# Zero fills on other engines, packed phase powers and a later state-space scan in a hybrid decoder block

## The chip, the cores and the metric

The kernel runs on one core of a Trainium2 chip. The metric is the device time of one execution in microseconds (us); the shown value is the median of three runs. The engines are called by the names of the profile: PE is TensorE, DVE is VectorE, ACT is ScalarE, POOL is GpSimd, SP is the engine that issues the weight loads.

## What is computed

One decoder layer on 512 tokens of width 1024, in float32. Only the parts that the change touches are shown.

```python
def hybrid_mixer(h, w_in, ...):
    proj = h @ w_in
    qa, ka, va, qd, kd, vd, u, g = jnp.split(proj, cuts, axis=-1)
    ya, _ = banded_attention(qa, ka, va, ...)      # branch A: window 128, 8 heads
    yb = dilated_attention(qd, kd, vd)             # branch B: three windows
    yc = s5_mixer(u, lam_re, lam_im, log_dt, ...)  # branch C: state space
    gates = jax.nn.sigmoid(g)
    merged = gates_0 * (ya @ w_branch_a) + gates_1 * (yb @ w_branch_b) + gates_2 * (yc @ w_branch_c)
    return merged @ w_out

def s5_mixer(u, ...):        # 32 groups of 16 channels, 64 complex states each
    ab_re, ab_im = mag * cos(li * dt), mag * sin(li * dt)
    # x_t = Abar x_{t-1} + Bbar u_t ;  y = Re(C x) + D u ;  then GELU and a gated unit
```

After the mixer come a residual, a norm, a gated convolution FFN of width 2816 and a final norm.

## The kernel before, in words

Every float32 weight is split into a high and a low part (`whi` by a copy on ACT, L66; `wlo` by a subtraction on DVE, L92), and each product of the layer is three matmuls (L171 to L173). Weights come in chunks of 256 columns; a chunk serves two **units** of work. A unit is 24 matmuls of 512 columns into one PSUM bank of the tag `mm` (there are two), and an evacuation of that bank on ACT: `pj` (a projection) for units 1 to 6 and 15 to 24, `th` (a gate, L983) for units 7 to 14.

The order of all work is written by hand. Each engine executes its instructions in the order in which the program emits them. `run` goes through the units; before unit u it emits one split of a coming chunk (`whi` on ACT, then `wlo` on DVE) and then the closures that `before(u, ...)` has put there. So a closure that waits on DVE holds up the split of the next unit, and the matmuls behind it.

The state-space branch runs as such closures, for four groups j of channels:

- `ssm_scalars` computes sine and cosine of the phase in tiny DVE instructions, mixed with the evacuations of the first norm (`hTl`, L345).
- `ssm_phase` squares the phase eight times on POOL (tiles `t`) and builds two tables from it (`eb`, `ea`, with the scratch `esc`). `ssm_e(j)` multiplies them to `E` on POOL.
- `ssm_cpow` multiplies the output weights by four powers on POOL (`vt`, `Vw`): three powers at its first step, the fourth at its second.
- `ssm_inj(j)`, `ssm_bd(j)` and `ssm_ob(j)` prepare the matrices. `ob` and `tz` are block-diagonal and must be zero outside the blocks.
- `ssm_m1(j)`: 16 matmuls into both PSUM banks of the tag `sc` (L677); four products `z` on DVE, which free those banks; two sums `z` on POOL; two scans on DVE (L687, L688); four more products on DVE, and `X` on POOL.
- `ssm_m2(j)`: matmuls with `tz`, `ob` and `X` (L711, L713) and the output `yS`.

Branch A (`attn_a`, four blocks of queries) uses the same two `sc` banks for its scores (L757). DVE adds the mask and takes the maximum (L764), ACT takes the exponentials (`smA`, L773), DVE divides. A step is one `st_(A[i])`.

All scratch tiles of 2 KB share one pool of 46 buffers (`slot`). A new tile takes over the buffer of an older one, and its first writer then waits for the last reader of that one.

Of the kernel before, what the change touches and what calls it, by code (L numbers as in the profile page):

```python
# [31 lines left out]
def hybrid_block(  # L32
# [36 lines left out]

# [1 line left out]
    class Chunk:  # L71
        """One raw load of up to [128, 2048] and its pieces of up to [128, 1024]."""

# [27 lines left out]
    def cols(w, c0, nl=1):  # L101
        """256 columns of a [1024, n] weight: eight k tiles in two pieces; get(k, c)."""

        def v(r):
            return r[:, :].rearrange("p (k n) -> p k n", n=256)

        wv = w.rearrange("(k p) n -> p k n", p=128)
        n = KD // nl
        c = Chunk([(lambda r, i=i: v(r)[:, i * n:i * n + n, :], wv[:, i * n:i * n + n, c0:c0 + 256])
                   for i in range(nl)],  # L110
                  [([128, 4, 256], [(lambda t: t[:, :, :], lambda r, i=i: v(r)[:, 4 * i:4 * i + 4, :])], None)
                   for i in range(2)])
        c.get = lambda k, a: tuple(t[:, k % 4, a * 128:a * 128 + 128] for t in c.p[k // 4])
        return c

    def qcols(w, cc):
        """Query columns of branch A, head pairs (j, j + 4) side by side, j = 2cc and 2cc + 1."""

# [17 lines left out]
    def rows(nk, n, loads):  # L136
        """n columns of a weight of nk k tiles, in pieces of 1024 / nk columns; get(k, c)."""
        pc = 1024 // nk

        def v(r):  # L140
            return r[:, :].rearrange("p (k n) -> p k n", n=n)

        c = Chunk([(lambda r, d=d: d(v(r)), s) for d, s in loads],
                  [([128, nk, pc], [(lambda t: t[:, :, :], lambda r, i=i: v(r)[:, :, i * pc:(i + 1) * pc])], None)
                   for i in range(n // pc)])

        def get(k, a):
            o = a * 128 % pc
            return tuple(t[:, k, o:o + 128] for t in c.p[a * 128 // pc])

        c.get = get
        return c

    def krows(w, k0, nk, c0, mk=None):
        """nk k tiles by 512 columns, as the moving operand; get(k)."""

# [24 lines left out]
    def tile_mm(ps, w, c, nk, act, o=slice(0, T)):  # L181
        """One [128, 512] output tile (or the tokens o of it), channels on partitions."""
        for k in range(nk):
            xh, xl = act(k)
            mm3(ps[:, o], w.get(k, c), xh[:, o], xl[:, o], k == 0, k == nk - 1)

# [1 line left out]
    units = []  # (chunk, closure emitting matmuls and evacuation)  # L188
    early = {}  # unit -> (chunk, pieces) to split before it, beyond the next chunk
    later = []  # closures to emit before the next unit  # L190
    plan = {}   # unit -> closures to emit before it

# [60 lines left out]

    queue = []       # small operations that fill the gaps of VectorE
    deferring = [False]
# [25 lines left out]

# [1 line left out]
    mhalf, epsv = cst([128, 1], "mhalf"), cst([128, 1], "epsv")  # L283
# [49 lines left out]
    def to_hT(pair, xs, gcol, dst, tags, hook=lambda: None):  # L333
        """Transposes two scaled token tiles (k -> view) into dst, times the norm's weight."""
        for kk in range(KD // 2):
# [38 lines left out]

# [1 line left out]
    P0_, P1_ = slice(0, 256), slice(256, 512)  # L376
# [20 lines left out]

# [1 line left out]
    maskA = cst([128, 256], "maskA")  # L399
# [23 lines left out]

# [1 line left out]
    cnt = [0]  # L425
# [11 lines left out]
    def exact_exp(o, i):  # L437
        """exp by reduction to |r| <= ln2 / 2 and its series, in float32."""
        c, k, r, p = ex
# [46 lines left out]
    def cmul(o, a, b, t, eng=None):  # L486
        """o = a * b for complex pairs; t: four scratch views."""
        tt(t[0], a[0], b[0], MUL, eng)
        tt(t[1], a[1], b[1], MUL, eng)
        tt(t[2], a[0], b[1], MUL, eng)  # L490
        tt(t[3], a[1], b[0], MUL, eng)
        tt(o[0], t[0], t[1], SUB, eng)
        tt(o[1], t[2], t[3], ADD, eng)

    pcol = cst([128, 48], "pcol")
    lr, li, ld, dcol = pcol[:, 0:16], pcol[:, 16:32], pcol[:, 32:48], vcol2[:, 32:48]
    dt_, mag, sn, cs, ar, ai, fr, fi, mag4 = (tiny() for _ in range(9))
    W, Vw, V0, V0b, DI, eb, ea = [], [], [], [], [], [], []
# [39 lines left out]
    def ssm_phase():  # L538
        ct = [tiny() for _ in range(4)]

        def csq(a):
            o = (tiny(), tiny())
            cmul(o, a, a, ct, G)
            return o

        pw = [csq(csq((cs, sn)))]
        for _ in range(6):
            pw.append(csq(pw[-1]))
        # phases of the chunks: 16 small steps times 8 large ones
        te, ta = slot([128, 2, 16, 16], name="eb"), slot([128, 2, 16, 8], name="ea")  # L550
# [55 lines left out]
    def expand(dst, src, j, scale=None):  # L606
        """Block diagonal over the two groups of each pair."""
        for g in range(2):
# [37 lines left out]

# [1 line left out]
    yS = []  # L648
# [72 lines left out]

# [1 line left out]
    def to_nat(src, name, strided=False):  # L723
        """[128 ch, 512] -> [128 keys, block, 128 ch]; strided: block r has the keys r, r + 4, ..."""
        pb = bank("pt")
# [74 lines left out]

# [1 line left out]
    zh, zl, yc = {}, {}, []  # L802
# [28 lines left out]

# [1 line left out]
    yb = {}  # L833
# [5 lines left out]
    def attn_b(hp):  # L839
        # statistics: [group, block, head of the pair]  # L840
        mx, nm, l = (cst([128, 3, 4, 2], f"{n}{hp}") for n in ("mxB", "nmB", "lB"))
# [24 lines left out]
        for i in range(4):  # L866
            for e in range(2):
                v = P0[i, e]
                S.activation(v, v, AF.Exp, bias=nm[:, 0, i, e:e + 1], scale=SCALE, accum_out=l[:, 0, i, e:e + 1])
        # group 0's statistics in the order of the other groups: (t mod 4, t div 4)  # L870
        nl = cst([128, 4, 2, 2], f"nlB{hp}")
# [102 lines left out]

# [1 line left out]
    m, th = {}, {}  # L976
# [48 lines left out]

# [1 line left out]
    x1 = []  # L1027
# [52 lines left out]

# [1 line left out]
    cpar = cst([128, 4, NF * 2], "cpar")  # L1082
# [62 lines left out]
    def down_unit(chunk, half, k0, n):  # L1145
        def fn():
# [11 lines left out]
            if final:  # L1158
                # the last token's part of this chunk goes to two banks of its own, 256 columns each
                order += [(NT - 1, k, c) for c in (slice(0, 256), slice(256, 512)) for k in range(n)]  # L1160
# [60 lines left out]

# [1 line left out]
    wup = bank("o", name="wup")  # L1223
# [33 lines left out]
    trans1(1, lambda: pump(2))  # L1257
    for j in range(4):
        OB[j] = [slot([128, 4, 4, 2, 16], name="ob") for _ in range(2)]
        TZ[j] = slot([128, 4, 4, 32], name="tz")  # L1260
        for t in (*OB[j], TZ[j]):
            G.memset(t, 0.0)
    masks_dve()
# [81 lines left out]
    before(5, lambda: ssm_inj(1), lambda: ssm_bd(2))  # L1345
    before(6, lambda: ssm_inj(2), lambda: ssm_bd(3), lambda: ssm_m1(0), st_(CP), lambda: ssm_e(1))
    before(7, lambda: ssm_inj(3), st_(A[0]))
    before(8, lambda: VA.append(to_nat(proj["vA"], "VA")), lambda: ssm_ob(0), st_(A[0]))
    before(9, lambda: ssm_m2(0), lambda: ssm_ob(1), lambda: ssm_m1(1), lambda: ssm_e(2))
    before(10, lambda: ssm_ob(2), st_(A[0]), st_(A[1]))  # L1350
    before(11, lambda: ssm_ob(3), st_(A[0]), st_(A[1]))
    before(12, lambda: ssm_m2(1), lambda: ssm_m1(2), lambda: ssm_e(3))
    before(13, st_(A[1]), st_(A[2]))
    before(14, st_(A[1]), st_(A[2]))
    before(15, st_(A[1]), lambda: ssm_m2(2), lambda: ssm_m1(3))
    before(16, st_(A[2]), st_(A[3]))
    before(17, st_(A[2]), st_(A[3]))
    before(18, st_(A[2]), lambda: ssm_m2(3))
    before(19, st_(A[3]))
    before(20, st_(A[3]), lambda: VB.setdefault(0, [to_nat(proj["vB", 0], "VB0")]))  # L1360
    before(21, st_(A[3]), lambda: VB[0].append(to_nat(proj["vB", 0], "VB1", True)))
    before(22, lambda: VB.setdefault(1, [to_nat(proj["vB", 1], "VB0")]))
# [44 lines left out]
```

## Time and profile before

| | before |
|---|---|
| median of three runs | 854.11 us (853.79 to 855.87) |
| profiled execution, first to last instruction (span) | 852.8 us |
| PE busy | 819.5 us, 96% of the span |
| DVE, ACT, POOL busy | 480.1, 352.1, 176.1 us |
| mean granted TensorE clock | 0.983 |

The profiled execution is timed by its span alone; the median of the runs lies 1.3 us above it. PE is busy nearly throughout, so the time can fall where PE stands still or runs at the lower clock.

### The profile page before, as it was taken

The page shows a single profiled execution, that of the slowest core. Times are in us where ns is not written, and L with a number is a line of the kernel's source. Part 1 is how long each engine was busy: PE and PEld are TensorE (multiplying, and loading weights), DVE is VectorE, ACT ScalarE, POOL GpSimd, SP SyncE. Part 2 cuts the span into 40 slices and gives each one's busy share as a digit, 9 for nine tenths or more (in the row PEclk, how much of TensorE's full clock was granted, in tenths as well). Part 3 has the DMA queues.
Part 4 walks back from the last instruction along what each step waited for, and adds up shares of the span by engine and source line. Part 5 has one row for each costly group of instructions (what it writes and reads, how often), then busy time and mean ns, then how long its engine had stood idle before and what let it go on. Part 6 is the DMA issues. An engine that isn't in the chain of part 4 may idle for free.

```text
span 852.8 us, 10536 instructions
## 1 busy us (share of the span) xinstructions
PE 819.5 (96%) x4085; PEld 678.7 (80%) x4085; DVE 480.1 (56%) x913; ACT 352.1 (41%) x661; POOL 176.1 (21%) x245
## 2 busy tenths in 40 slices
PE   8799669999999999999999999999999999999996
PEld 7788556877787788888887898888888888888885
DVE  5996579777224655645474456555566665422313
ACT  6347145445434554442344244444444444312212
POOL 6379876243000000005250000000000000002002
PEclk9899969999999999999999999999999999999999
DMA  8332011111233131332335124222222223323402
GB/s 237 99 99 84 16 50 51 50 49 50 72 77 105 51 99 50 100 99 74 125 100 196 50 64 135 97 91 90 92 91 92 93 98 123 125 72 99 148 0 99
DMA packets 68278, 76.60 MB, mean 90 GB/s; under 512 B 8161, under 2 KB 55557, under 8 KB 68229
## 3 DMA queue, kind: packets, MB, share of 16 engines
q1 hardware_dynamic: 67972, 75.89, 28.3%
q8 instruction: 32, 0.52, 0.3%
q0 software_dynamic: 256, 0.05, 0.1%
q14 instruction: 18, 0.14, 0.1%
HBM read 73.81 MB, written 2.12 MB: 89 GB/s over the span
## 4 chain that ended last, share of the span: by engine, by line
PE 72%; DVE 13%; POOL 8%; issue 3%; ACT 2%; DMA 1%; SPq 0%; POOLq 0%; DVEq 0%; ACTq 0%
PE up L172 9%; PE up L171 9%; PE up L173 9%; PE mm L171 7%; PE mm L172 7%; PE mm L173 7%; PE acc L178 6%; PE acc L179 6%; PE acc L177 6%; POOL t L279 2%; DVE z L279 2%; DVE wlo L92 2%; DVE t L271 1%; POOL esc L279 1%; DVE z L687 1%
## 5 line engine op out<-in xcount | busy, mean ns | idle before, releaser
L92 DVE TENSOR_TENSOR wlo<-raw,whi 128x1024 fp32r<-128x1024 f32 (+1 forms) x126 | 153.1, 1223 | 152.1 <-ACT whi L66 152.0
L66 ACT ACTIVATE whi<-raw 128x1024 fp32r<-128x1024 f32 (+1 forms) x126 | 127.4, 1023 | 58.4 <-PE acc L179 56.2
L171 PE MATMUL up<-hTh,whi 128*128 128x512 f32 (+1 forms) x384 | 142.7, 372 | 0.0
L172 PE MATMUL up<-hTl,whi 128*128 128x512 f32 (+1 forms) x384 | 142.6, 371 | 0.0
L173 PE MATMUL up<-hTh,wlo 128*128 128x512 f32 (+1 forms) x384 | 142.6, 371 | 0.0
L171 PE MATMUL mm<-hTh,whi 128*128 128x512 f32 (+1 forms) x336 | 134.5, 400 | 0.0
L172 PE MATMUL mm<-hTl,whi 128*128 128x512 f32 (+1 forms) x336 | 131.2, 390 | 0.0
L173 PE MATMUL mm<-hTh,wlo 128*128 128x512 f32 (+1 forms) x336 | 130.9, 390 | 0.0
L275 DVE SCALAR_TENSOR_TENSOR cc<-up,cpar,cc 128x511 f32<-128x511 f32 x88 | 65.9, 749 | 97.3 <-ACT cc L1101 95.8
L171 PEld LDWEIGHTS up<-hTh,whi 128*128 128x128 f32 x384 | 72.3, 188 | 12.6
L173 PEld LDWEIGHTS up<-hTh,wlo 128*128 128x128 f32 x384 | 72.3, 188 | 12.6
L172 PEld LDWEIGHTS up<-hTl,whi 128*128 128x128 f32 x384 | 72.3, 188 | 12.3
L171 PEld LDWEIGHTS mm<-hTh,whi 128*128 128x128 f32 x336 | 64.7, 193 | 15.5 <-issue 2.3
L173 PEld LDWEIGHTS mm<-hTh,wlo 128*128 128x128 f32 x336 | 64.4, 192 | 13.2
L172 PEld LDWEIGHTS mm<-hTl,whi 128*128 128x128 f32 x336 | 64.7, 193 | 11.9
L177 PE MATMUL acc<-whi,gh 128*128 128x512 f32 x172 | 66.9, 389 | 0.0
L178 PE MATMUL acc<-wlo,gh 128*128 128x512 f32 x172 | 66.9, 389 | 0.0
L179 PE MATMUL acc<-whi,gl 128*128 128x512 f32 x172 | 66.9, 389 | 0.0
L279 POOL TENSOR_TENSOR x<-x,gfin 128x512 f32<-128x512 f32 x4 | 5.2, 1289 | 296.8 <-ACT acc L1040 296.8
L1101 ACT ACTIVATE cc<-up,cpar 128x512 f32<-128x512 f32 x44 | 34.3, 779 | 61.2 <-PE up L173 60.4
L983 ACT ACTIVATE th<-mm 128x512 f32<-128x512 f32 x24 | 14.2, 594 | 76.2 <-PE mm L173 58.5
L66 ACT ACTIVATE gh<-cc 128x512 fp32r<-128x512 f32 x22 | 13.9, 632 | 59.4 <-DVE cc L279 59.4
(299 smaller groups left out, 1291.2 us busy)
## 6 DMA issues: line engine op xcount, KB each, us to landing
raw<-in_w_up_dram SPq DMA_DIRECT2D x22, 1024.0 KB, 5.1
raw<-in_w_in_dram SPq DMA_DIRECT2D x18, 1024.0 KB, 5.1
raw<-in_w_down_dram SPq DMA_DIRECT2D x10, 1024.0 KB, 5.0
x<-in_x_dram SPq DMA_DIRECT2D x8, 512.0 KB, 6.2
raw<-in_w_in_dram SPq DMA_DIRECT2D x8, 512.0 KB, 5.2
raw<-in_w_out_dram SPq DMA_DIRECT2D x4, 1024.0 KB, 5.1
raw<-in_w_branch_a_dram SPq DMA_DIRECT2D x4, 512.0 KB, 6.7
raw<-in_w_branch_c_dram SPq DMA_DIRECT2D x2, 1024.0 KB, 5.0
```

The costliest lines, as they stand in the source:

```text
L66: S.activation(o, i, AF.Copy)
L92: (lo_eng or V).tensor_tensor(view(lo), r, view(hi).bitcast(F32), op=ALU.subtract)
L171: PE.matmul(ps, wh, xh, start=first, stop=False)
L172: PE.matmul(ps, wh, xl, start=False, stop=False)
L173: PE.matmul(ps, wl, xh, start=False, stop=last)
L177: PE.matmul(ps, xh, wh, start=first, stop=False)
L178: PE.matmul(ps, xh, wl, start=False, stop=False)
L179: PE.matmul(ps, xl, wh, start=False, stop=last)
L275: emit(lambda: V.scalar_tensor_tensor(o, a, s, b, op0=op0, op1=op1))
L279: emit(lambda: (eng or V).tensor_tensor(o, a, b, op=op))
L983: S.activation(t, ps, AF.Tanh, scale=0.5)
L1101: S.activation(dst, ps, AF.Identity, bias=cpar[:, 3, f:f + 1], scale=cpar[:, 2, f:f + 1])
```

## The change

Three edits. The eight `ob` and four `tz` tiles are zeroed at the very start, on DVE (`memset`) and ACT (a copy with scale 0), and no more on POOL after the first norm. The squaring of the phase works on cosine and sine packed side by side: four POOL instructions for a squaring where there were six. And the scans are emitted later: `ssm_m1(0)` moves from unit 6 to unit 9, and each later `ssm_m1`, `ssm_m2` and `ssm_e` three units further on, so that `ssm_m2(3)` stands at unit 21. Comments are taken out as well.

```diff
-    dt_, mag, sn, cs, ar, ai, fr, fi, mag4 = (tiny() for _ in range(9))
+    dt_, mag, ar, ai, fr, fi, mag4 = (tiny() for _ in range(7))
+    cssn = tiny(32)
+    cs, sn = cssn[:, 0:16], cssn[:, 16:32]
...
     def ssm_phase():
-        ct = [tiny() for _ in range(4)]
+        ct, sq = tiny(), tiny(32)
 
         def csq(a):
-            o = (tiny(), tiny())
-            cmul(o, a, a, ct, G)
+
+            o = tiny(32)
+            tt(sq, a, a, MUL, G)
+            tt(ct, a[:, 0:16], a[:, 16:32], MUL, G)
+            tt(o[:, 0:16], sq[:, 0:16], sq[:, 16:32], SUB, G)
+            tt(o[:, 16:32], ct, ct, ADD, G)
             return o
 
-        pw = [csq(csq((cs, sn)))]
+        pk = [csq(csq(cssn))]
         for _ in range(6):
-            pw.append(csq(pw[-1]))
+            pk.append(csq(pk[-1]))
+        pw = [(v[:, 0:16], v[:, 16:32]) for v in pk]
...
+    for j in range(4):
+        OB[j] = [slot([128, 4, 4, 2, 16], name="ob") for _ in range(2)]
+        TZ[j] = slot([128, 4, 4, 32], name="tz")
+        for t in OB[j]:
+            V.memset(t, 0.0)
+        S.activation(TZ[j][:, :, :, :].rearrange("p a b c -> p (a b c)"), epsv.to_broadcast([128, 512]), AF.Copy,
+                     scale=0.0)
     wup = bank("o", name="wup")
...
     trans1(1, lambda: pump(2))
-    for j in range(4):
-        OB[j] = [slot([128, 4, 4, 2, 16], name="ob") for _ in range(2)]
-        TZ[j] = slot([128, 4, 4, 32], name="tz")
-        for t in (*OB[j], TZ[j]):
-            G.memset(t, 0.0)
     masks_dve()
...
-    before(6, lambda: ssm_inj(2), lambda: ssm_bd(3), lambda: ssm_m1(0), st_(CP), lambda: ssm_e(1))
+    before(6, lambda: ssm_inj(2), lambda: ssm_bd(3), st_(CP))
...
-    before(9, lambda: ssm_m2(0), lambda: ssm_ob(1), lambda: ssm_m1(1), lambda: ssm_e(2))
+    before(9, lambda: ssm_m1(0), lambda: ssm_ob(1), lambda: ssm_e(1))
...
-    before(12, lambda: ssm_m2(1), lambda: ssm_m1(2), lambda: ssm_e(3))
+    before(12, lambda: ssm_m2(0), lambda: ssm_m1(1), lambda: ssm_e(2))
...
-    before(15, st_(A[1]), lambda: ssm_m2(2), lambda: ssm_m1(3))
+    before(15, st_(A[1]), lambda: ssm_m2(1), lambda: ssm_m1(2), lambda: ssm_e(3))
...
-    before(18, st_(A[2]), lambda: ssm_m2(3))
+    before(18, st_(A[2]), lambda: ssm_m2(2), lambda: ssm_m1(3))
...
-    before(21, st_(A[3]), lambda: VB[0].append(to_nat(proj["vB", 0], "VB1", True)))
+    before(21, st_(A[3]), lambda: VB[0].append(to_nat(proj["vB", 0], "VB1", True)), lambda: ssm_m2(3))
```

On POOL, between the last weight split of the first norm (`wlo`) and the first squaring, before; the fills in front of these rows repeat the pair `ob`, `tz` four times in all:

```order
L1262 MEMSET ob 128x512 x2
L1262 MEMSET tz 128x512
L279 TENSOR_TENSOR t_669<-t_146 128x16
L279 TENSOR_TENSOR t_670<-t_145 128x16
L279 TENSOR_TENSOR t_671<-t_146,t_145 128x16
L279 TENSOR_TENSOR t_672<-t_145,t_146 128x16
L279 TENSOR_TENSOR t_673<-t_669,t_670 128x16
L279 TENSOR_TENSOR t_674<-t_671,t_672 128x16
```

The same place on POOL with the change:

```order
L92 TENSOR_TENSOR wlo<-raw,whi 128x1024 x2
L279 TENSOR_TENSOR t_669<-t_150 128x32
L279 TENSOR_TENSOR t_668<-t_150 128x16
L279 TENSOR_TENSOR t_670<-t_669 128x16
L279 TENSOR_TENSOR t_670<-t_668 128x16
```

The fills are gone from there, and a squaring is four rows where it was six; eight squarings make 32 instructions where they made 48.

On POOL at the end of the third power of `ssm_cpow`, before (`z` and `X` belong to `ssm_m1(0)`, the last `vt` and `Vw` are the fourth power):

```order
L279 TENSOR_TENSOR Vw<-vt 128x256 x2
L279 TENSOR_TENSOR z<-z 128x512 x2
L696 MEMSET X 128x4 x2
L279 TENSOR_TENSOR X<-z,xt 128x4x127
L279 TENSOR_TENSOR X<-z 128x4x127
L279 TENSOR_TENSOR vt<-Vw,t_147 128x256
L279 TENSOR_TENSOR vt<-Vw,t_148 128x256 x2
L279 TENSOR_TENSOR vt<-Vw,t_147 128x256
L279 TENSOR_TENSOR Vw<-vt 128x256 x2
```

The same place with the change:

```order
L279 TENSOR_TENSOR vt<-Vw,t_145 128x256
L279 TENSOR_TENSOR vt<-Vw,t_146 128x256 x2
L279 TENSOR_TENSOR vt<-Vw,t_145 128x256
L279 TENSOR_TENSOR Vw<-vt 128x256 x2
L279 TENSOR_TENSOR z<-z 128x512 x2
L703 MEMSET X 128x4 x2
```

The fourth power now stands in front of the first scan's sums `z`.

On ACT at units 7 and 8, with the semaphores that each instruction waits for, before (`th` is the evacuation of unit 7, `whi` the next split, `VA` and `ob` belong to unit 8):

```order
L983 ACTIVATE th<-mm 128x512 [waits DVE_49,PE_49]
L66 ACTIVATE whi<-raw 128x1024
L66 ACTIVATE VA<-pt 128x512 [waits PE_49,Pool_49]
L66 ACTIVATE ob<-Vw 64x16x16 [waits Pool_49]
L66 ACTIVATE ob<-Vw 64x16x16
L68 ACTIVATE ob<-Vw 64x16x16 [waits Pool_49]
```

The same place with the change:

```order
L990 ACTIVATE th<-mm 128x512 [waits PE_49,Pool_49]
L66 ACTIVATE whi<-raw 128x1024 [waits DVE_49]
L66 ACTIVATE VA<-pt 128x512 [waits PE_49,Pool_49]
L66 ACTIVATE ob<-Vw 64x16x16 x2
```

The buffers of the pool have moved on: `th` of unit 7 waited for a DVE instruction of the first scan, and now waits for POOL. The count that it waits for is that of the first of the two `Vw` of the fourth power.

## Rows read from the trace of the kernel before

**Rows 1.** Busy time of each engine by stretch, granted clock, DMA

```profile
core 0: us, PE busy (x) PEld busy (x) DVE busy (x) ACT busy (x) POOL busy (x), PEclk, DMA share, GB/s
100.00:110.00 10.00, 1.56 (x9) 1.07 (x8) 7.17 (x7) 1.90 (x3) 5.98 (x9) 0.84 0.00 0
110.00:120.00 10.00, 5.98 (x18) 4.81 (x19) 7.62 (x26) 3.91 (x17) 9.92 (x10) 0.50 0.33 105
600.00:700.00 100.00, 100.00 (x443) 82.81 (x442) 58.08 (x73) 44.18 (x57) 0.00 (x0) 1.00 0.30 95
```

**Rows 2.** Waits of PE up to 240 us: total us, times, longest

```profile
PE sc L757 <- DVE mxA L764: 14.9, 3, 12.5
```

**Rows 3.** DVE in order of time: start, us, instruction, idle before

```profile
0.89 0.17 DVE L312 MEMSET vrow<- 48x128 f32 x1
5.66 0.15 DVE L330 TENSOR_SCALAR stat<-stat 128x1 f32<-128x1 f32 x1 [4.61 <-ACT junk L355]
...
21.86 7.91 DVE L271 TENSOR_SCALAR t<-t 128x16 f32<-128x16 f32 x1
24.10 5.68 DVE L345 SCALAR_TENSOR_TENSOR hTl<-nt,vcol,hTh 128x256 fp32r<-128x256 f32 x1
```

**Rows 4.** POOL in order of time, fills and first squarings

```profile
19.01 5.13 POOL L92 TENSOR_TENSOR wlo<-raw,whi 128x1024 fp32r<-128x1024 f32 x2 [1.57 <-DVE whi L91]
...
29.23 0.51 POOL L1262 MEMSET tz<- 128x512 f32 x1
47.58 0.41 POOL L279 TENSOR_TENSOR t<-t 128x16 f32<-128x16 f32 x2 [17.84 <-DVE t L279]
...
66.11 0.12 POOL L555 MEMSET eb<- 128x16 f32 x1
```

**Rows 5.** POOL in order of time, powers, first scan and a later scan

```profile
97.84 2.36 POOL L279 TENSOR_TENSOR vt<-Vw,t 128x256 f32<-128x256 f32 x4
...
101.54 2.47 POOL L279 TENSOR_TENSOR z<-z 128x512 f32<-128x512 f32 x2
...
111.08 3.34 POOL L279 TENSOR_TENSOR vt<-Vw,t 128x256 f32<-128x256 f32 x4
...
167.73 1.66 POOL L279 TENSOR_TENSOR X<-z,xt 128x508 f32<-128x508 f32 x1 [3.39 <-DVE xt L279]
```

**Rows 6.** DVE in order of time, first two scans and branch A

```profile
102.83 2.27 DVE L687 TENSOR_TENSOR_SCAN z<-a,z 128x512 f32<-128x512 f32 x1 [9.73 <-POOL z L279]
...
115.44 0.28 DVE L764 CUSTOM_DVE_ANT_0 smA<-sc,maskA 128x128 f32<-128x128 f32 x1
...
122.51 2.52 DVE L269 TENSOR_SCALAR smA<-smA,lA 128x128 f32<-128x128 f32 x8
125.24 1.23 DVE L92 TENSOR_TENSOR wlo<-raw,whi 128x1024 fp32r<-128x1024 f32 x1 [0.21 <-ACT whi L66]
...
130.75 2.48 DVE L279 TENSOR_TENSOR z<-sc,E 128x512 f32<-128x512 f32 x4
...
160.37 2.48 DVE L279 TENSOR_TENSOR z<-sc,E 128x512 f32<-128x512 f32 x4
```

**Rows 7.** PE in order of time, units 8 and 9

```profile
114.02 1.64 PE L757 MATMUL sc<-pj 64*128 64x128 f32 x8 [12.46 <-DVE mxA L764]
...
123.47 0.38 PE L711 MATMUL o<-us,tz 128*128 128x128 f32 x2
...
126.14 1.95 PE L677 MATMUL sc<-us,inj 128*128 128x128 f32 x16
```

**Rows 8.** ACT in order of time, first microseconds and evacuations

```profile
4.48 1.06 ACT L355 ACTIVATE junk<-x 128x1024 f32<-128x1024 f32 x1 [2.24 <-DMA x<-in_x_dram]
...
108.10 0.60 ACT L983 ACTIVATE th<-mm 128x512 f32<-128x512 f32 x1 [12.61 <-DVE z L279]
108.59 1.05 ACT L66 ACTIVATE whi<-raw 128x1024 fp32r<-128x1024 f32 x1
...
162.68 0.60 ACT L983 ACTIVATE th<-mm 128x512 f32<-128x512 f32 x1 [3.42 <-PE mm L173]
```

## The prediction, made before the change was timed

> **What bounds the kernel now.** I read the busy time by stretch first, then who PE waits for, then the engines named there in order of time. PE runs full at clock 1.00 through the long later stages, where 443 matmuls take 100 us, or 0.226 us each [rows 1]; nothing is to be had there. Between 100 and 110 us it is busy for 1.56 us, and in the ten after that for 5.98 us at a granted clock of 0.50, the lower level of 1.2 GHz, after standing idle [rows 1]. The waits say for whom: 14.9 us behind DVE's L764, 12.5 of them in one piece [rows 2], the piece in front of the scores at 114.02 [rows 7].
>
> That hole is a queue on two engines. The second set of L764 (115.44) stands on DVE behind the whole of `ssm_m1(0)`; its scan at 102.83 had waited 9.73 us for POOL's sums `z` [rows 6]; and these start at 101.54, because POOL works without a pause from 47.58, through squarings, tables, `E` and three powers [rows 4, 5]. POOL's start at 47.58 is DVE's: it waits 17.84 us for sine and cosine.
>
> DVE in turn lost time before that. An instruction of 16 columns, L271, starts at 21.86 and takes 7.91 us, and the `hTl` behind it takes 5.68 [rows 3]. POOL's weight splits end at 24.14 (19.01 + 5.13) and its last fill at 29.74 (29.23 + 0.51) [rows 4]; L271 ends at 29.77. So DVE stands still until POOL's fills are through. The Trainium skill ("SBUF — State Buffer", Who interferes with whom) says that VectorE and GpSimd share a port pair, which one holds for a whole instruction while the other is fully blocked; the rows agree.
>
> **The fills.** Off POOL: DVE is free at 24.14, 5.6 us sooner, and all that DVE does next, sine and cosine included, comes 5.6 us sooner. POOL starts at 47.58 - 5.6 = 42.0. If the stall were not the fills' doing, this would be 0.
> At their new place: DVE has nothing between its fill of `vrow` at 0.89 + 0.17 = 1.06 and L330 at 5.66 [rows 3]. Eight fills of 512 columns cost at least 8 x 0.51 = 4.1 us (POOL's fill of that size) [rows 4] and at most 8 x 4 x 0.17 = 5.4 us (the fill of 128 columns, four times): end at 5.1 to 6.5, so 0 to 0.8 us late. ACT idles for 2.24 us before 4.48; four instructions of 0.60 us make 2.4 [rows 8], 0 to 0.2 us late. I take 0. The cover is the wait for the first tokens; without it the start would be 4 us later.
> The Trainium skill ("VectorE: DVE Perf Modes", Zero memsets can be issued as uint32) gives one cycle per element, and 0.96 GHz in its Specifications; an estimate from that page is 0.53 us a fill and 4.3 us for eight, which would also fit. No row shows a DVE fill of this size.
>
> **The squarings.** 48 instructions fill POOL from 47.58 to 66.11, 0.386 us each on average, while the first two took 0.41 together, 0.2 each [rows 4]; the rest is waiting on DVE's own instructions. Sixteen fewer save 3.2 us (at 0.2) to 6.2 us (at 0.386). I take 3.2: DVE's instructions remain, and what POOL does instead has to wait for them as well.
>
> **The order on POOL.** One power takes 101.54 - 97.84 = 3.7 us, of which 2.36 are its four products; the fourth power's products took 3.34 [rows 5]. So the fourth power in front of `z` costs 3.7 to 5.2 us; I take 3.7 and add 0.6, half of a DVE split (1.23) [rows 6] that now meets the powers. The first of its two `Vw` ends 0.7 us, half of 3.7 - 2.36, before it does: 101.54 - 5.6 - 3.2 + 3.7 + 0.6 - 0.7 = 96.3.
>
> **What is late next.** For that `Vw` ACT's `th` of unit 7 now waits, as the order shows, and behind it stands `whi` of the coming chunk; DVE's `wlo` waits for `whi`, and the second L764 stands behind `wlo`. From start of `th` to end of `whi` 1.5 us (108.10 to 109.64) [rows 8]: 97.8. `wlo` 1.2: 99.0. From L764 to the end of the divisions, with the exponentials on ACT between, 125.03 - 115.44 = 9.6 [rows 6]: 108.6. One more `wlo` 1.2, and the products `z` of unit 9 start at **109.8**. Before, unit 9 has its `z` at 130.75 [rows 6]: **21.0 us sooner**.
>
> PE is not later than this chain. It stood ready for the scores of unit 8 at 114.02 - 12.46 = 101.56. It gets there 5.6 sooner (the stall) and 1.95 sooner (L677 is gone from unit 6) [rows 7]: 94.0; with 1.6 for scores and 24 x 0.226 = 5.4 for the unit it wants the `sc` banks for L677 at 101.0, and DVE frees them at 99.0 + 0.9 = 99.9. The two are within a microsecond or two, so the chain and not PE sets the time, barely.
>
> From there one scan follows the other as before: `z` at 130.75 and 160.37, 29.6 us apart [rows 6], with the same steps of branch A between. So 21.0 us hold until unit 18.
>
> **What comes back.** At unit 9 before, PE had done `m1` of two groups and `m2` of one; now one `m1`. The rest is done later, in units where PE has no wait to hide it: one `m1`, 1.95 us, and one `m2`, 126.14 - 123.47 = 2.7 us [rows 7]. **+4.6**.
> A second new wait of ACT is in unit 12: its `th` now takes a buffer that POOL's first `X` frees. Against `z` at 160.37, `th` wanted to start 2.3 us later (162.68) [rows 8] and that `X` ends 9.0 us later (167.73 + 1.66) [rows 5]: 6.7 us held. The other `mm` bank covers one unit, 5.4 us. Between 0 and 6.7; I take the difference, **+1.3**. In units 15 and 18 the like wait falls a unit later, behind its `X`.
>
> **Sum.** 852.8 - 21.0 + 4.6 + 1.3 = 837.7 us of span; the median lies 1.3 above the span: **839.0 us**.
>
> **The rivals.**
> *More, since each squaring gives back what it took.* POOL's instructions took turns with DVE's in that stretch, so a missing one could save its 0.386. For it: the average. Against: DVE's instructions stay. Saves 6.2 instead of 3.2, and the chain starts 3.0 sooner: 836. If the tables run free of DVE as well, down to the point where PE binds (about 2 more): 834. The Trainium skill's rule of the first holder (the SBUF page above) fits this too.
> *Less, since the powers stay slow.* The fourth power at 5.2, fills 0.8 late, the saving of 5.6 cut by half because POOL meets other DVE instructions: 1.5 + 0.8 + 2.8 = 5.1 more: 844. Had the stall not been the fills' doing at all: 839 + 5.6 = 844.6.
> *Slower: ACT parked behind the scans.* ACT executes in order, and its evacuations now take buffers that POOL and DVE free late. If 6.7 us were exposed in each of units 9, 12, 15 and 18, PE would lose 26.8 us, in place of 1.3: 864.5. It turns the result from 4.1 us (16.4 / 4) a time onward. Against it: there are two `mm` banks, and before, ACT waited 12.61 us at 108.10 in the same way [rows 8].
> *No change.* The chain would have to give up all: the fourth power and the parked `whi` would have to cost 15 us, where 5.2 and 1.5 are the bounds.
>
> **How the numbers follow.** The sum as forecast (835 to 843) 0.50; more 0.20 (831 to 835); less 0.21 (843 to 850); no change 0.03; slower 0.06. The range leaves out a little at each end: 832 to 847. A measurement of this kernel cannot tell less than about 0.3%, or 2.5 us, from no change. Faster by more than that 0.91, within it 0.03, slower 0.06.
>
> **What would show it.** The L271 behind the splits ends near 24.2. DVE's fills end before L330, which stays near 5.7. POOL's first squaring is at 42, `eb` is cleared near 57 (15 us later, not 18.5), and the first `z` of POOL comes after the fourth power. ACT's `th` of unit 7 starts near 96 and names POOL. DVE's first `z` is near 110, and PE's long wait at L757 has gone, with waits of 1 to 3 us at L677 and L757 around 100 to 123 in its place. The forecast is wrong if `th` of unit 7 starts outside 91 to 101, if L330 is later than 6.5, or if PE stands still for more than 4 us anywhere between 100 and 200.

## The result, and the profile after

| | before | after |
|---|---|---|
| median, runs side by side on one chip | 854.99 us (853.79 to 856.15, 4 runs) | 839.94 us (839.67 to 840.54, 4 runs) |
| ratio, 95% interval | | 0.9834 (0.9806 to 0.9863) |
| span of the profiled execution | 852.8 us | 838.7 us |
| mean granted TensorE clock | 0.983 | 0.994 |

The kernel is 1.7% faster; the forecast was 839.0. The lines of the changed kernel are numbered 7 higher from the phase onward (L764 is L771, L757 is L764, L677 is L684, L711 is L718, L983 is L990).

The busy time by stretch, in the columns of [rows 1]: the hole is filled. From 100 to 120 us PE is busy for 18.0 us, where it was for 7.5.

```profile
100.00:110.00 10.00, 8.41 (x39) 7.54 (x40) 6.51 (x24) 8.15 (x28) 0.00 (x0) 0.83 0.33 107
110.00:120.00 10.00, 9.58 (x46) 6.64 (x45) 9.70 (x12) 5.24 (x10) 5.70 (x7) 1.00 0.00 0
```

Whom PE waits for, up to 240 us [rows 2], the longer ones: the single wait of 12.5 us is gone, and small ones stand in many places. The first row is a wait at the start (`nt`, the transposes of the first norm, 1.4 us before); the run swap below comes back to it.

```profile
PE nt L340 <- DVE x L366: 3.4, 1, 3.4
PE sc L684 <- DVE mxA L771: 3.3, 1, 3.3
PE sc L764 <- DVE mxA L771: 3.0, 2, 1.6
PE o L800 <- ACT pTA L66: 2.2, 2, 1.8
PE sc L764 <- DVE z L279: 2.1, 2, 1.6
```

DVE in order of time [rows 3, 6]. The fills end before the statistics need DVE (5.81). L271 still shows a stall, but of 2.33 us and not 7.91. The products `z` of units 9, 12 and 15 are the last three rows; before, they stood at 130.75, 160.37 and 190.59.

```profile
1.11 4.27 DVE L1234 MEMSET ob<- 128x512 f32 x8
5.81 0.15 DVE L330 TENSOR_SCALAR stat<-stat 128x1 f32<-128x1 f32 x1 [0.43 <-ACT junk L355]
8.46 2.63 DVE L366 TENSOR_SCALAR x<-x,stat 128x512 f32<-128x512 f32 x1
22.77 2.33 DVE L271 TENSOR_SCALAR t<-t 128x16 f32<-128x16 f32 x1
...
101.03 0.28 DVE L771 CUSTOM_DVE_ANT_0 smA<-sc,maskA 128x128 f32<-128x128 f32 x1
102.19 0.17 DVE L279 TENSOR_TENSOR esA<-sink,nmA 128x8 f32<-128x8 f32 x1
105.71 0.17 DVE L279 TENSOR_TENSOR lA<-lA,esA 128x8 f32<-128x8 f32 x1 [3.35 <-ACT smA L780]
106.15 1.66 DVE L269 TENSOR_SCALAR smA<-smA,lA 128x128 f32<-128x128 f32 x8
108.86 2.48 DVE L279 TENSOR_TENSOR z<-sc,E 128x512 f32<-128x512 f32 x4
138.51 2.49 DVE L279 TENSOR_TENSOR z<-sc,E 128x512 f32<-128x512 f32 x4
170.58 2.48 DVE L279 TENSOR_TENSOR z<-sc,E 128x512 f32<-128x512 f32 x4
```

POOL in order of time [rows 4, 5]: the squarings take 10.9 us, the fourth power (95.22) stands in front of the sums `z` (110.29), and POOL is now idle from 98.96 to 110.29.

```profile
8.47 2.34 POOL L92 TENSOR_TENSOR wlo<-raw,whi 128x1024 fp32r<-128x1024 f32 x1
...
43.17 10.96 POOL L279 TENSOR_TENSOR t<-t 128x32 f32<-128x32 f32 x32 [18.10 <-DVE t L279]
54.08 0.13 POOL L562 MEMSET eb<- 128x16 f32 x1
...
95.22 2.36 POOL L279 TENSOR_TENSOR vt<-Vw,t 128x256 f32<-128x256 f32 x4
97.54 1.42 POOL L279 TENSOR_TENSOR Vw<-vt 128x256 f32<-128x256 f32 x2
110.29 2.51 POOL L279 TENSOR_TENSOR z<-z 128x512 f32<-128x512 f32 x2 [11.33 <-DVE z L279]
```

PE in order of time [rows 7], units 15 and 18. The last row is the first matmul of `ssm_m2` in unit 18, the end of the chain that the prediction follows.

```profile
172.61 1.63 PE L764 MATMUL sc<-pj 64*128 64x256 f32 x8 [1.59 <-DVE z L279]
183.43 1.82 PE L764 MATMUL sc<-pj 64*128 64x256 f32 x8 [1.45 <-DVE mxA L771]
...
191.85 0.49 PE L718 MATMUL o<-us,tz 128*128 128x128 f32 x2
```

The same row of the kernel before, in its own trace:

```profile
210.44 0.49 PE L711 MATMUL o<-us,tz 128*128 128x128 f32 x2
```

ACT in order of time [rows 8]: its fills (2.14), `th` of unit 7 (98.31), `th` of unit 12 parked behind `X` (147.56), and in unit 14 an evacuation `pTA` parked behind POOL's `E` for 5.79 us, with the exponentials of branch A (from L778 on) behind it. The row of `th` of unit 7 names PE, but the last matmul of that unit ended at 91.56 (91.16 + 0.40); `th` starts as the first `Vw` of the fourth power ends (98.25), so it waits for POOL, as the order said.

```profile
2.14 2.17 ACT L1235 ACTIVATE tz<-epsv 128x512 f32<-128x512 f32 x4
4.63 1.06 ACT L355 ACTIVATE junk<-x 128x1024 f32<-128x1024 f32 x1 [0.32 <-DMA x<-in_x_dram]
...
98.31 0.60 ACT L990 ACTIVATE th<-mm 128x512 f32<-128x512 f32 x1 [11.22 <-PE mm L173]
...
147.56 0.60 ACT L990 ACTIVATE th<-mm 128x512 f32<-128x512 f32 x1 [10.17 <-POOL X L279]
...
158.21 0.60 ACT L66 ACTIVATE pTA<-pt 128x512 f32<-128x512 f32 x1 [5.79 <-POOL E L279]
158.71 0.20 ACT L778 ACTIVATE esA<-esA 128x8 f32<-128x8 f32 x1
```

The account along the chain: `z` of unit 9 is 21.9 us sooner (130.75 to 108.86), that of unit 12 also 21.9 (160.37 to 138.51), that of unit 15 20.0 (190.59 to 170.58), `ssm_m2` of unit 18 18.6 (210.44 to 191.85). From there to the end of the span it is 642.4 us before and 646.9 after, 4.5 more. 18.6 - 4.5 = 14.1 us, the difference of the spans. The medians lie 15.1 us apart; of the 1.0 us between the two figures 0.6 is that the profiled execution of the change was the slowest of its four (840.54).

### The profile page after: what moved, and what is told of

It is laid out like the page before. It is cut to its first block, busy times and chain, and to the rows that moved or that the text cites. A ratio compares the mean times of both kernels' runs of the same rounds, so it can differ in the third digit from the quotient of the medians.

```text
span 838.7 us, 10519 instructions
## 1 busy us (share of the span) xinstructions
PE 814.7 (97%) x4085; PEld 676.3 (81%) x4085; DVE 479.3 (57%) x921; ACT 353.8 (42%) x665; POOL 168.2 (20%) x217
## 4 chain that ended last, share of the span: by engine, by line
PE 82%; DVE 9%; ACT 2%; issue 2%; POOL 2%; DMA 1%; SPq 0%; POOLq 0%; DVEq 0%; ACTq 0%
PE up L172 10%; PE up L173 10%; PE up L171 10%; PE mm L171 9%; PE mm L173 9%; PE mm L172 9%; PE acc L178 6%; PE acc L179 6%; PE acc L177 6%; DVE wlo L92 1%; DMA x<-in_x_dram 1%; DVE z L279 1%; PE sc L896 1%; PE nt L340 1%; POOL th L279 1%
## 5 line engine op out<-in xcount | busy, mean ns | idle before, releaser
L171 PE MATMUL mm<-hTh,whi 128*128 128x512 f32 (+1 forms) x336 | 132.3, 394 | 0.0
L172 PE MATMUL mm<-hTl,whi 128*128 128x512 f32 (+1 forms) x336 | 129.4, 385 | 0.0
L171 PEld LDWEIGHTS up<-hTh,whi 128*128 128x128 f32 x384 | 72.4, 189 | 12.5
L171 PEld LDWEIGHTS mm<-hTh,whi 128*128 128x128 f32 x336 | 63.3, 188 | 14.5 <-issue 2.5
L990 ACT ACTIVATE th<-mm 128x512 f32<-128x512 f32 x24 | 14.3, 594 | 71.1 <-PE mm L173 58.2
```

Source lines behind the costliest of these rows:

```text
L171: PE.matmul(ps, wh, xh, start=first, stop=False)
L172: PE.matmul(ps, wh, xl, start=False, stop=False)
L990: S.activation(t, ps, AF.Tanh, scale=0.5)
```

## The experiments

All numbers are medians with their range and the ratio to the kernel before, run beside it.

**One part at a time.** The kernel before with the fills alone moved (p_fills):

```diff
+        for t in OB[j]:
+            V.memset(t, 0.0)
+        S.activation(TZ[j][:, :, :, :].rearrange("p a b c -> p (a b c)"), epsv.to_broadcast([128, 512]), AF.Copy,
+                     scale=0.0)
     wup = bank("o", name="wup")
...
-        for t in (*OB[j], TZ[j]):
-            G.memset(t, 0.0)
```

> Kernel before with the zero fills alone moved. Chain theory (POOL's start, set by DVE, sets the time of everything up to unit 18): the stall of L271 goes, POOL's first squaring starts about 4.5 us sooner (5.6 less the 1 us that the changed kernel lost at L366), all later work follows and nothing is given back: 850.5 us, and PE's wait at L757 stays near 12 us. Rival (fills matter only with the scans out of the way, since PE's wait there swallows the gain): 854 to 855 us.

849.00 us (848.5 to 849.81), 0.9934 (0.9919 to 0.9949). POOL's first squaring is at 42.27 and `z` of unit 9 at 124.36, 6.4 us sooner. The wait for the scores stays whole, as the waits of PE show:

```profile
PE sc L757 <- DVE mxA L764: 15.3, 3, 12.4
```

So the fill stall was real: of the 6.4 us, 6.1 come through to the end of the span (846.7), while the hole of 12.5 us is not its doing. Behind `ssm_m2` of unit 18 nothing is given back: 642.3 us are left from there, as before (642.4).

The kernel before with packed squarings alone (p_packed):

```diff
+            tt(sq, a, a, MUL, G)
+            tt(ct, a[:, 0:16], a[:, 16:32], MUL, G)
+            tt(o[:, 0:16], sq[:, 0:16], sq[:, 16:32], SUB, G)
+            tt(o[:, 16:32], ct, ct, ADD, G)
```

> Kernel before with the packed squarings alone. Chain theory: squarings take 11 us instead of 18.5, but tables and E take about 3.5 us more since DVE's instructions are still there: POOL's first z comes 4 us sooner, 851 us. Rival More (each squaring gives back what it took and nothing is lost behind it): 7.6 us, 847.4 us. Rival Less (POOL meets other DVE instructions and the saving is cut by half): 1.6 us, 853.4 us.

850.48 us (845.78 to 853.82, ten runs), 0.9946 (0.9924 to 0.9968). The runs fell into two groups, 845.8 to 849.0 and 852.0 to 853.8, and the profiled one belongs to the upper. The granted clock goes with them, 0.986 to 0.988 in the lower and 0.981 to 0.984 in the upper; which of the two brings the other no run shows. The median lies between the groups, so the time can't tell the three expectations apart. In the trace, from the first squaring to the end of the third power is 100.12 - 49.20 = 50.9 us, where it was 101.54 - 47.58 = 54.0: packing saves 3.0 there, near the 3.2 of the prediction. But the first squaring came 1.6 us later than before (49.20), behind a scaling L366 that took 2.64 us; the run swap below is about that row.

The kernel before with the later scans alone (p_late):

```diff
-    before(6, lambda: ssm_inj(2), lambda: ssm_bd(3), lambda: ssm_m1(0), st_(CP), lambda: ssm_e(1))
+    before(6, lambda: ssm_inj(2), lambda: ssm_bd(3), st_(CP))
...
-    before(9, lambda: ssm_m2(0), lambda: ssm_ob(1), lambda: ssm_m1(1), lambda: ssm_e(2))
+    before(9, lambda: ssm_m1(0), lambda: ssm_ob(1), lambda: ssm_e(1))
```

> Kernel before with the later scans alone. Chain theory: third power ends at 101.5 as before, the first Vw of the fourth at 104.6, th of unit 7 then, whi to 106.1, wlo to 107.3, second set of L764 to the end of the divisions 6.8 us, wlo, first z of unit 9 at 115.3, 15.5 us sooner than before; one m1 and one m2 (4.6) and ACT's parked th (3.3) come back: 847.4 us. The three parts alone then sum to 4.5 + 4 + 7.6 = 16 us, close to the 15 measured for all. Rival (the three parts are worth their gain only together): the sum of the three single gains is under 10 us or over 20.

848.96 us (847.91 to 850.10), 0.9937 (0.9920 to 0.9954). PE's long wait is halved and has moved in front of the injection matmuls, and DVE's `z` of unit 9 comes 14.5 us sooner. First the waits of PE, then DVE:

```profile
PE sc L677 <- DVE mxA L764: 6.3, 1, 6.3
```

```profile
116.23 2.47 DVE L279 TENSOR_TENSOR z<-sc,E 128x512 f32<-128x512 f32 x4
```

Of these 14.5 us 11.2 are left at `ssm_m2` of unit 18 (199.24) and 6.7 at the end of the span (846.1): what is given back later comes with this edit. The three parts alone make 0.66%, 0.54% and 0.63%, in sum 1.83%; together they gave 1.66%. The intervals are as wide as the difference, so the runs agree with parts that add, and can't show it more closely. In microseconds they are worth 5.9, 4.4 (2.8 in the run p_packed_swap below, whose five runs lie together) and 5.9, in sum 14.6 to 16.1, against 15.1 for all, so neither under 10 nor over 20 as the rival wanted. The prediction's sum has 5.6 for the fills, 3.2 for the squarings and 6.3 for the rest of its 15.1.

**Is the order on POOL the binding chain?** The changed kernel, its fourth power computed twice (power_twice):

```diff
-            cmul(nxt, prev, [bc(ar), bc(ai)], [t[:, i] for t in vt for i in range(2)], G)
+            for _ in range(2 if k == 3 else 1):
+                cmul(nxt, prev, [bc(ar), bc(ai)], [t[:, i] for t in vt for i in range(2)], G)
```

> Changed kernel with the fourth power computed twice on POOL (same values, six POOL instructions more, 3.7 us). Chain theory: the first Vw that th of unit 7 waits for ends 3.7 us later, and all up to unit 18 with it: 843.6 us. Rival (PE or DVE sets the time there and POOL has slack): below 841 us.

843.59 us (843.38 to 844.88), 0.9873 (0.9858 to 0.9888), 3.7 us above the change. `z` of unit 9 moves from 108.86 to 111.99, and PE's wait at the injection matmuls grows from 3.3 to 6.8:

```profile
111.99 2.47 DVE L279 TENSOR_TENSOR z<-sc,E 128x512 f32<-128x512 f32 x4
```

`th` of unit 7 moves with it, and its row now names POOL:

```profile
101.44 0.60 ACT L991 ACTIVATE th<-mm 128x512 f32<-128x512 f32 x1 [14.82 <-POOL Vw L279]
```

The second power is the first's work again (3.7 us by [rows 5]). POOL's first squaring came 0.5 us sooner in this execution (42.67, L366 at 0.48); counted from there, `z` is 3.6 us later. What POOL does more appears one to one: the chain binds and nothing covers it. Whether less work on POOL would win as much, this run does not show.

**Is the cover of the fills what the prediction said?** The changed kernel, each `ob` filled twice (fills_twice):

```diff
-        for t in OB[j]:
+        for t in OB[j] * 2:
```

> Changed kernel with each of the eight DVE fills done twice (4.27 us more in the first microseconds). Theory (the cover is the wait for the first tokens, of which 0.43 us is left before L330): L330 at 9.6 instead of 5.8, all that follows 3.8 us later: 843.7 us. Rival (slack in the prologue, as the transposes wait for weights anyway): 840 to 841.5 us.

845.44 us (845.3 to 846.94), 0.9887 (0.9872 to 0.9903), 5.5 more than the change. DVE in order of time:

```profile
1.11 8.60 DVE L1234 MEMSET ob<- 128x512 f32 x16
9.63 0.09 DVE L330 TENSOR_SCALAR stat<-stat 128x1 f32<-128x1 f32 x1
...
113.12 2.48 DVE L279 TENSOR_TENSOR z<-sc,E 128x512 f32<-128x512 f32 x4
```

The statistics come 3.8 us later, `z` of unit 9 4.3 us later. The wait for the first tokens hides the eight fills and 0.4 us more. Another 1.6 us is lost by `ssm_m2` of unit 18 (197.71, 5.9 later); there PE's granted clock was 0.86 from 190 to 200 us, 1.00 in the change. What lowered it stays open.

**The start.** The changed kernel, with the scaling L366 emitted ahead of the split that POOL shares (swap):

```diff
-    cu[0].split(0, V, G)
     scale1(1)
+    cu[0].split(0, V, G)
```

> Changed kernel with the scaling of the second token tile (L366) put ahead of the first weight split, so that POOL's wlo cannot start in front of it. Chain theory: L366 takes 0.48 us instead of 2.63, POOL's first squaring starts 0.5 to 1.0 us sooner (43.2 before, 42.7 in a run without the collision), and the time falls by as much: 839.0 to 839.5 us. Rival (the start of the prologue has slack): 839.9 us and the first squaring at 43.2.

840.28 us (839.65 to 841.84), 0.9833 (0.9817 to 0.9849): no difference that can be told. The step itself worked, as DVE's row shows (2.63 before the swap); the first squaring is at 42.60 and `z` of unit 9 at 108.15, 0.7 sooner than in the profiled execution of the change.

```profile
7.90 0.48 DVE L366 TENSOR_SCALAR x<-x,stat 128x512 f32<-128x512 f32 x1 [0.67 <-POOL stat L331]
```

The collision is a matter of the single execution. Five further runs below and above begin like the change (power_twice, e_later, pta_free, e_later_hold, all_moved), and in their traces L366 takes 0.47 or 0.48 us and the first squaring stands between 42.29 and 42.69. So the swap takes away what the median execution of the change may not have had, which would explain that the medians agree; the span of the profiled one (838.0) is the 0.7 us under that of the change.

The same swap in p_packed (p_packed_swap) asks whether that collision separates its two groups of times:

> Kernel before with the packed squarings and with L366 put ahead of the first weight split. The packed squarings alone gave runs from 845.8 to 853.8 us. Theory (in some executions L366 is blocked for 2 us by the wlo that POOL starts in front of it, which puts the whole chain later): the runs lie close together, within 1.5 us, near 848 us. Rival (the spread comes from a later stage): as wide as without the swap.

851.89 us (850.84 to 852.18, five runs), 0.9961 (0.9949 to 0.9974). The runs lie within 1.4 us, as the theory had it, but at the upper end and not near 848: L366 takes 0.49 and the time is still nearly that of the upper group. So the collision alone does not separate the groups. No run shows a trace of the lower group, and the cause stays open. From the first squaring to the end of the third power it is 51.0 us here too.

**The parked ACT.** The changed kernel, `ssm_e(1)` to `ssm_e(3)` one unit later (e_later):

```diff
-    before(12, lambda: ssm_m2(0), lambda: ssm_m1(1), lambda: ssm_e(2))
-    before(13, st_(A[1]), st_(A[2]))
+    before(12, lambda: ssm_m2(0), lambda: ssm_m1(1))
+    before(13, lambda: ssm_e(2), st_(A[1]), st_(A[2]))
```

> Changed kernel with ssm_e(1), (2), (3) one unit later, so that th of unit 12 takes a buffer that PE freed long before, and not the one that POOL's X frees. Theory (the parked th of unit 12 costs what PE waits at o L800 and behind it, 1.8 us, and up to 3 us with the units after): 837 to 838.3 us, th of unit 12 at about 141 instead of 147.6. Rival (the wait only moves to pTA, which waits for the same X, and to the scans after it): 839.5 to 840 us.

840.18 us (839.84 to 840.47), 0.9829 (0.9815 to 0.9843). `th` of unit 12 is free and waits for PE's matmuls only, 7.2 us sooner; from `z` of unit 12 to that of unit 15 it is still 32.06 us, as in the change (32.07). ACT in order of time:

```profile
140.38 0.60 ACT L990 ACTIVATE th<-mm 128x512 f32<-128x512 f32 x1 [3.56 <-PE mm L173]
...
157.64 0.60 ACT L66 ACTIVATE pTA<-pt 128x512 f32<-128x512 f32 x1 [5.81 <-POOL E L279]
```

The wait of `th` thus costs nothing that can be measured. The second row is the one that stays: `pTA` of unit 14 behind POOL's `E`.

That wait taken away, by `ssm_e(2)` in unit 12 ahead of `ssm_m1(1)` (pta_free):

```diff
-    before(12, lambda: ssm_m2(0), lambda: ssm_m1(1), lambda: ssm_e(2))
+    before(12, lambda: ssm_m2(0), lambda: ssm_e(2), lambda: ssm_m1(1))
-    before(15, st_(A[1]), lambda: ssm_m2(1), lambda: ssm_m1(2), lambda: ssm_e(3))
-    before(16, st_(A[2]), st_(A[3]))
+    before(15, st_(A[1]), lambda: ssm_m2(1), lambda: ssm_m1(2))
+    before(16, lambda: ssm_e(3), st_(A[2]), st_(A[3]))
```

> Changed kernel with ssm_e(2) emitted ahead of ssm_m1(1) in unit 12 and ssm_e(3) in unit 16, so that neither th of unit 12 waits for POOL's X nor pTA of unit 14 for POOL's E(2). New theory (from the changed kernel's trace and the run e_later: the exponentials of unit 14 start at 158.7, 1.85 us after their input, since pTA in front of them on ACT waits for E(2)): first z of unit 15 comes 30.2 us after that of unit 12 instead of 32.07, near 168.7, PE's wait of 1.6 us behind it goes, and the time falls to 838.0 to 838.4 us. Rival (PE is late there by itself): 839.5 to 840.2 us.

840.06 us (839.13 to 840.18), 0.9823 (0.9809 to 0.9836). DVE in order of time:

```profile
131.64 4.61 DVE L269 TENSOR_SCALAR smA<-smA,lA 128x256 f32<-128x256 f32 x8
...
141.11 2.49 DVE L279 TENSOR_TENSOR z<-sc,E 128x512 f32<-128x512 f32 x4
...
169.72 2.48 DVE L279 TENSOR_TENSOR z<-sc,E 128x512 f32<-128x512 f32 x4
```

From `z` of unit 12 to unit 15 it is now 28.6 us, 3.5 less; from unit 9 (108.24) to unit 12 it is 32.9, 3.2 more. Eight divisions of the same shape took 2.19 us in the change and 4.61 here, where POOL works on `E` beside them. The loss has only changed places. Of the 3.5 us 0.8 is `esA` of that stretch, which takes 0.17 us where it took 0.98 in the change, beside POOL's `E`.

**Holding the scratch.** Three runs keep the scratch `vt` of the powers alive by two fills of one element, so that `th` of unit 7 doesn't take a buffer of the fourth power. In e_later_hold they stand in unit 10:

```diff
+        for t in vt:
+            G.memset(t[:, 0, 0:1, 0:1], 0.0)
+        yield
...
+    before(10, lambda: ssm_e(1), st_(CP), lambda: ssm_ob(2), st_(A[0]), st_(A[1]))
```

> As e_later, and vt kept until unit 10 by two one-element fills, so that th of unit 7 takes another buffer and no longer waits for the fourth power. Chain theory: th, whi, wlo and the second set of L771 come when PE has the scores (near 94 instead of 101); the exponentials stay behind ob(0), which needs the fourth power: divisions end near 105.7 instead of 107.8, first z of unit 9 at 106.8, 2 us sooner, and PE's wait at L684 goes: 2 us under e_later. Rival (the wait moves to ob(0) and nothing is gained): same time as e_later within 0.5 us.

844.13 us (841.49 to 845.29), 0.9871 (0.9851 to 0.9891): 4 us more than the change, where 2 less were expected. `th` of unit 7 came at 91.14, and `z` of unit 9 at 106.98, as meant. But POOL reaches the two fills only after its `E` (126.69), and DVE's mask step waits for the buffer behind them; first POOL, then DVE:

```profile
126.69 0.13 POOL L611 MEMSET vt<- 128x1 f32 x2
```

```profile
126.86 0.42 DVE L774 CUSTOM_DVE_ANT_0 smA<-sc,maskA 128x256 f32<-128x256 f32 x1 [2.98 <-POOL vt L611]
```

So `z` of unit 12 comes 33.1 us after that of unit 9 (29.65 in the change). Behind unit 15 another 1.9 us are lost; PE's granted clock was 0.86 from 180 to 190 us there, 1.00 in the change, and the cause stays open.

The combination of this with the swap and with `ob(0)` behind the exponentials of unit 8 (comb) has the same fault, and a second one:

> All three edits, and ob(0) behind the exponentials of unit 8. Chain theory: nothing on ACT or DVE stands behind the fourth power any more, z of unit 9 comes when PE has done m1, near 100 to 101 instead of 108.9, and the waits of PE between 95 and 190 us (about 10 us with the slow clock) mostly go: 831 to 834 us. Rival (DVE and POOL with their own load set the distance of 29.65 us from scan to scan, so that PE is late again from unit 12 on): 836 to 838 us.

839.58 us (838.91 to 842.56), 0.9829 (0.9809 to 0.9849), where 831 to 834 was expected. The profiled execution is the slowest of the four (842.56). In it DVE waits 3.28 us for the fills, and `z` of unit 12 comes 33.0 us after that of unit 9 (29.7 in the change). And `z` of unit 9 is at 107.40, where 100 to 101 was expected: PE's granted clock was 0.50 from 60 to 65 us (1.00 in e_later_hold), and `th` of unit 7, whose row names PE, came at 94.66 instead of 91.14. What lowered the clock stays open.

The last run (all_moved) takes pta_free, puts the two fills right behind `ssm_m1(0)` in unit 9, `ssm_e(1)` in unit 10, and `ob(0)` behind the exponentials of unit 8:

```diff
-    before(8, lambda: VA.append(to_nat(proj["vA"], "VA")), lambda: ssm_ob(0), st_(A[0]))
-    before(9, lambda: ssm_m1(0), lambda: ssm_ob(1), lambda: ssm_e(1))
-    before(10, lambda: ssm_ob(2), st_(A[0]), st_(A[1]))
+    before(8, lambda: VA.append(to_nat(proj["vA"], "VA")), st_(A[0]), lambda: ssm_ob(0))
+    before(9, lambda: ssm_m1(0), st_(CP), lambda: ssm_ob(1))
+    before(10, lambda: ssm_e(1), lambda: ssm_ob(2), st_(A[0]), st_(A[1]))
```

> pta_free, and ssm_e(1) in unit 10, vt held until POOL's X of the first scan by two one-element fills, ob(0) behind the exponentials of unit 8, and the prologue as in the changed kernel. Chain theory: second set of L771 near 94, exponentials end near 99.7, divisions near 102, first z of unit 9 near 104.3 instead of 108.9; from there 29.65 and 30.2 us from scan to scan: 834 to 836 us, less if PE follows. Rival (the run comb: what is won before the first scan is lost before the second, at a spacing of 33 us): 838.5 to 840 us.

834.65 us (833.42 to 836.65), 0.9764 (0.9745 to 0.9783). It beats both kernels, the change by about 5 us. The time is as expected, the way to it is not: the distances from scan to scan are 33.1 and 28.1 us, where 29.65 and 30.2 were expected. `z` of unit 9 is 5.0 us sooner than in the change, that of unit 12 only 1.6, that of unit 15 5.5:

```profile
103.82 2.48 DVE L279 TENSOR_TENSOR z<-sc,E 128x512 f32<-128x512 f32 x4
...
136.96 2.49 DVE L279 TENSOR_TENSOR z<-sc,E 128x512 f32<-128x512 f32 x4
...
165.06 2.48 DVE L279 TENSOR_TENSOR z<-sc,E 128x512 f32<-128x512 f32 x4
```

## Why the prediction was right, and where its terms were off

The forecast and its mechanism held: the stall was the fills' (p_fills), POOL's queue sets the time of unit 9 (power_twice), and moving the scans turned one long wait into small ones (p_late). 839.0 was forecast and 839.94 measured. Its signs held as well: `th` of unit 7 at 98.31, L330 at 5.81, and no stand-still of PE above 3.3 us between 100 and 200. That the sum was right to a microsecond is partly luck, since terms that were off by 1 to 3 us balanced: 21.9 us were won up to unit 9 and not 21.0, and 3.3 were lost from there to unit 18 and not 1.3.

**The fills.** Right: DVE's eight end at 5.38 and L330 is 0.15 us late, ACT's `junk` likewise. fills_twice shows that the named cover is nearly the whole of it. L271 again ends with POOL's split, as the prediction had it, at 25.10 and 25.07 (19.95 + 5.12); but the split itself ended 0.9 us later than the 24.14 of before. "POOL starts at 42.0" was 1.2 us too early: 43.17. About half of this is L366, which in this execution ran into POOL's split (8.46, 2.63 us, beside `wlo` at 8.47 for 2.34); where it takes 0.48, the start is at 42.3 to 42.7. On one point the rows go beyond the rule that the prediction cites for the stall, which is one of a single instruction: before, L271 stood behind the rest of a split and twelve fills in a row, from 21.86 to 29.77 [rows 3, 4], and did not get in between them.

**The squarings.** "I take 3.2" was too much: the net is 1.9. The section itself fell by 7.6 us, from 18.5 to 10.9, more than even the rival *More* had. But the next section grew by 5.7. The busy times from the clearing of `eb` to the end of the third power show it (columns as in [rows 1]); first before, then after:

```profile
66.11:101.54 35.43, 34.01 (x192) 29.09 (x190) 20.23 (x32) 18.56 (x46) 35.20 (x71) 0.95 0.18 60
```

```profile
54.08:95.22 41.14, 40.62 (x239) 34.54 (x238) 31.30 (x55) 23.60 (x56) 40.90 (x71) 1.00 0.23 77
```

The same 71 instructions of POOL take 35.4 us beside 20.2 us of DVE's work, and 41.1 beside 31.3. POOL got ahead, so DVE's work of that time now lies beside its tables and powers. p_packed has a like 40.0, and p_fills, where POOL and DVE move together, 35.3. That DVE's work is what lengthens POOL's is read from these four rows; no run varied it by itself. The reason that the prediction gave for its value, that the work behind still has to wait for DVE, was right; its size wasn't. Rival *More* fell for the same reason.

**The order on POOL.** 3.6 us were taken from the end of the third power to the first `Vw` of the fourth; it was 3.0 (95.22 to 98.25, with half of the last 1.42). So `th` of unit 7 came at 98.31 and not 96.3. power_twice shows that this chain binds.

**What is late next.** From `th` to `z` 13.5 us were reckoned and 10.55 measured. The term that was off most is "the divisions with the exponentials on ACT between", 9.6 us: from L771 to their end it is 6.8. Before, POOL multiplied `E` beside them, as these rows of DVE from the trace of before show; now POOL is idle there.

```profile
116.85 0.98 DVE L279 TENSOR_TENSOR esA<-sink,nmA 128x8 f32<-128x8 f32 x1
...
121.20 1.04 DVE L279 TENSOR_TENSOR lA<-lA,esA 128x8 f32<-128x8 f32 x1 [3.37 <-ACT smA L773]
```

And POOL beside them, in the same trace:

```profile
116.75 1.05 POOL L279 TENSOR_TENSOR E<-eb,ea 128x512 f32<-128x512 f32 x1
...
121.15 1.06 POOL L279 TENSOR_TENSOR et<-eb,ea 128x512 f32<-128x512 f32 x1
```

`esA` starts behind POOL's `E` and ends with it (117.83 and 117.80), `lA` behind `et` in the same way (122.24 and 122.21). After, `esA` takes 0.17 instead of 0.98, `lA` 0.17 instead of 1.04, the divisions 1.66 instead of 2.52: 2.5 of the 2.8 us. The price was taken from a stretch in which another engine was in the way, and the change itself took that engine away. pta_free shows the reverse, 2.19 to 4.61. The Trainium skill ("SBUF — State Buffer", Who interferes with whom) says that a VectorE instruction with two inputs in SBUF contends with a GpSimd instruction that reads SBUF, and that the later one is blocked until the earlier one is done; the ends of these rows agree.

Summed: 1.2 + 1.3 - 0.6 - 3.0 = -1.1 against 109.8, and `z` of unit 9 is at 108.86.

**What comes back.** "+4.6" for one `m1` and one `m2` was right: 4.5 from unit 18 to the end, and the same 4.5 in p_late, where p_fills has none. "+1.3" for `th` of unit 12 named the wrong place. It did wait, by 10.17 us, but e_later gives it free and gains nothing, as if the second `mm` bank covered it all; no run shows the cover by itself. What was lost is in units 12 to 15, 1.9 us, and in units 15 to 18, 1.4 us. The first is the time by which the exponentials of unit 14 start after their input: 158.71, while DVE's `esA` ended at 156.84. `pTA` stands in front of them, parked behind `E` of the next group, which the change moved along with the scan. pta_free takes this away and gains 3.5 us in that stretch, but loses 3.2 in the one before, so the time stays. For the 1.4 us the rows of PE name two waits, 1.59 and 1.45 us; no experiment took these apart.

**The rivals.** *Less* fell with p_fills: the stall was the fills'. Of its parts, the fourth power took 3.74 us (95.22 to 98.96) and not 5.2, L330 was 0.15 late and not 0.8, and of the 5.6 us at POOL's start 1.2 were missing and not 2.8. *Slower* had its mechanism right, ACT parked behind POOL, but it cost time in one place and not four, and 1.9 us there. *No change* fell with every part.

## What to carry to other kernels

A duration from the trace holds for what runs beside it: before such a row goes into a sum, look at what the other engine does in that stretch and whether the change leaves it there. Where an engine is made faster, the saving is read at the end of its whole queue, since it meets other work sooner. And a step that moves takes its buffers with it: read for each queue behind it whose last reader the next instruction waits for, and test that wait by removing it, as one of 10.17 us cost nothing here, and another of 5.79 us put 1.9 us on the chain, whose removal in turn moved the loss elsewhere. Read more than one execution, too: the collision of 2 us at the start stood in the profiled execution of the change and in two of the ten other traces with that order.

## What was unexpected of the hardware

- A DVE instruction of 8 columns can cost as much as a POOL instruction of 512 (the rows of `esA` and `lA` above): small size is no protection against a busy neighbour.
- After standing idle for 3.3 us, PE took 3.40 us for the 16 injection matmuls that took 1.95 [rows 7], with a granted clock of 0.58 from 101.58 to 104.98, mostly the lower level of 1.2 GHz:

```profile
101.58 3.40 PE L684 MATMUL sc<-us,inj 128*128 128x128 f32 x16 [3.27 <-DVE mxA L771]
```

- Two fills of a single element, 0.13 us on POOL together, parked DVE for 2.98 us, since it stood behind POOL's queue and held a buffer.
